# Hybrid encoder layer on one core: input projections in split halves, gate blocks between convolutions, a fixed order for the second sequence's queries, 80 up-blocks before the downs

## The chip, the cores and the metric

The kernel runs on one core of a Trainium2 chip. The metric is the device time of one execution in microseconds (us), lower is better, as the median of several executions. Engines: PE is TensorE (matmuls), DVE is VectorE, ACT is ScalarE, POOL is GpSimd, SP is SyncE, which here only issues DMAs.

## The reference

Two sequences of 256 tokens go through one encoder layer. Cut to what matters:

```python
h = layer_norm(concat([meta, x]))                 # 16 + 256 tokens, 1024 wide
proj = h @ w_in                                   # z | xBC | dt | c_q | c_kv | k_rope
y_ssm = rms_norm(ssd(silu(conv5(xBC)), dt) * silu(z))        # 16 heads, both directions
y_attn = rms_norm(attention(c_q @ w_uq, c_kv @ w_ukv, k_rope))  # 8 heads
h = layer_norm(alpha * h + concat([y_ssm, y_attn]) @ w_out)
# PEER: q = h @ w_q; 8 heads, product keys, top-16 twice, then
s1, s2 = q[..., 0] @ sub_keys[0].T, q[..., 1] @ sub_keys[1].T
experts, g = top16(top16(s1) + top16(s2))         # 16 of 16384 experts, softmax weights
act = gelu(u_tab[experts] . h);  out = sum(g * act * v_tab[experts])
y = layer_norm(alpha * h + out)[meta:]
```

All arrays are float32.

## The kernel before

**Two kinds of matmul.** `mm1` multiplies float32 tiles as they were loaded. `mm3` multiplies *halves*: a tile is split into a high half (an ACT cast to fp32r) and a low half (a DVE subtraction, raw minus high), and three fp32r matmuls, high by high, high by low, low by high, replace one float32 matmul. `stream` loads a 512 KB block of weights and splits it; its tiles are `wraw` (3 buffers), `whi` and `wlo` (2 each). `whole` loads a block for `mm1` into whichever of these seven buffers is next.

**First part.** Tokens are normalised and transposed into `hT` (channels on partitions, 272 columns). `win(s)` makes the input projections of sequence s: 18 blocks of w_in, eight accumulated matmuls each over 272 columns, and 8 half-blocks of w_z for the gates (4 chunks, 2 tiles of 256 columns each). Of the 18, 12 go through a five-tap convolution on DVE (four instructions at L415). `mla(s)` is the attention, `ssd(s)` the state-space part, `wout(s)` the output projection with the layer norm that follows, `queries(s)` the 16 query heads (projection, scores, `top16` on DVE). `mix` interleaves generators at fixed rates and the scheduler of the framework then orders each engine; the stages here are win(0) with mla(0), win(1) with ssd(0), wout(0) with mla(1) and ssd(1), queries(0) with the rest of these, and wout(1) with the routes of tiles 1 and 0 (`route`: a second top-16 and index arithmetic, nearly all DVE).

**Second part, in an order written by hand.** Of the four tiles of 128 tokens, tile 0 (`GT`) gathers its experts by indirect DMA (paced by `pace`, 257 gather steps in all, an accumulated rate per unit); tiles 1 to 3 (384 columns, `x1T_hi`, `x1T_lo`) instead go densely through all 16384 experts: an *up* (`umul`) multiplies 128 experts of u with the 384 tokens (24 fp32r matmuls and a gelu), a *down* (`outer`) multiplies their values with 128 experts of v. There are 128 of each. A `unit` is one step of the order: it may hold one up, and one hot step: a g step (`gunits`: 16 per tile, one-hot tables on DVE and 16 small f16 matmuls that build the dense gate matrix, written to DRAM as `gd`) or a route step (`rsteps`, 6 per tile). Up results of the first groups of 8 stay in SBUF (`RES` 2 groups) or are spilled to DRAM (`SPILL` groups, `hdr`). Before, the 16 g steps of tile 1 run with the 16 query heads of sequence 1 and an up in every second unit; then 6 route units, 16 g units, 6 and 16 again with an up each; then a flush, 12 more ups, and with 8 x (2 + 6) = 64 ups made, the loop of the downs starts with the other 64 ups inside.

Of the kernel before, what the change touches and what calls it, by code (L numbers as in the profile page):

```python
# [8 lines left out]
F32 = mybir.dt.float32  # L9
# [25 lines left out]
SPILL = 6  # L35
# [9 lines left out]
GDOWN, GUP = 0.8, 2.0  # L45
FIN = 116
EROWS, MRATE = 4, 0.8
HP = 400
RM, RS2, RM3, RS3 = 0.7, 0.6, 1.0, 0.6
# [3 lines left out]
DEL = (3, 0)  # L53
# [3 lines left out]
W0 = (12, 13, 14, 15, 16, 17, 8, 9, 10, 11, 0, 1, 2, 3, 4, 5, 6, 7)  # L57
W1 = (12, 8, 9, 13, 14, 15, 16, 17, 10, 11, 0, 1, 2, 3, 4, 5, 6, 7)
R0, RS = 1.05, 0.55
# [3 lines left out]
def build(ctx, tc, i, o):  # L63
# [176 lines left out]
    xbc, yn = [], []  # L240
    for _ in range(2):
        xbc.append(blk_tile([128, 12, L]))
        yn.append(blk_tile([128, 12, T]))
# [158 lines left out]

    def win(s):
        H = hT[s]
# [43 lines left out]
        for c in range(4):  # L448
            w = []
            for kh in range(2):  # L450
                w.append(whole(i["w_z"][2 * c + kh], 1024).rearrange("p (k m) -> p k m", k=4))
            for t in range(2):
                sl = slice(NM + t * 128, NM + (t + 1) * 128)
                pz = pm()[:, :256]
                mm1(pz, [(H[:, k, sl], w[k // 4][:, k % 4]) for k in range(8)])
                th = phw.tile([128, L], F32, name="th", bufs=2)[:, :256]
                nc.scalar.activation(th, pz, AF.Tanh, scale=0.5)
                zt = phw.tile([128, L], F32, name="cv")[:, :256]
                nc.vector.scalar_tensor_tensor(zt, th, 1.0, pz, op0=OP.add, op1=OP.mult)
                nc.sync.dma_start(zd[2 * s + t][:, c * 256:(c + 1) * 256], zt)  # L460
                yield 1

# [203 lines left out]

    def wout(s):
        kk = (8, 9, 10, 11, 0, 1, 2, 3, 4, 5, 6, 7)

        def prod(acc, t, n, w):  # L670
            k = kk[n]
            mm1(acc, [(yn[s][:, k, t * 128:(t + 1) * 128], w[:, (k % 2) * 512:(k % 2 + 1) * 512])], n_done=n, n_all=12)

        acc = [wa() for t in range(2)]
        for n in range(0, 12, 2):
            w = whole(i["w_out"][0, kk[n] // 2], 1024)
            for t in range(2):
                prod(acc[t], t, n, w)
                prod(acc[t], t, n + 1, w)
            yield 1  # L680
        h = blk_tile([128, 3, D])
        for t in range(2):
            nc.sync.dma_start(h[:, t], hd[2 * s + t])
        nc.scalar.dma_start(h[:, 2], bcast_row(i["ln1_g"], D))
        if s == 0:
            lq["b"] = gp.tile([128, D], F32, name="x1g")
            nc.scalar.dma_start(lq["b"], bcast_row(i["ln1_b"], D))
# [6 lines left out]
        for t in range(2):  # L694
            for n in range(12):
                prod(acc[t], t, n, ws[n // 2])
                if n % 4 == 3:
                    yield 1
# [581 lines left out]
```

## Time and profile before

| | |
|---|---|
| times | 1818.65, 1817.49, 1813.78 us; median 1817.49 |
| profiled execution | 1815.48 us, of which 1813.6 us is the span shown in the trace |
| PE busy | 1709.2 us (94%) |
| DVE busy | 1317.7 us (73%) |
| ACT busy, POOL busy | 639.0, 434.1 us |
| DMA | 433.83 MB, mean 239 GB/s |

The trace is one execution on one core. A busy PE is one that has matmuls in flight. The stages by their place in the span: 20.7 to 306 projections of both sequences, 306 to 357 wout(0), 357 to 511 the rest of attention and state space and the queries of sequence 0, 511 to 553 wout(1), 553 to 586 its norms and the routes of tiles 1 and 0, 586 to about 936 the 52 units with ups and the others, 936 to 1009 twelve ups and the passage to the downs, 1009 to 1750 the downs, then the finish.

### The profile page before, as it was taken

The page shows a single profiled execution, that of the slowest core. Times are in us where ns is not written, and L with a number is a line of the kernel's source. Part 1 is how long each engine was busy: PE and PEld are TensorE (multiplying, and loading weights), DVE is VectorE, ACT ScalarE, POOL GpSimd, SP SyncE. Part 2 cuts the span into 40 slices and gives each one's busy share as a digit, 9 for nine tenths or more (in the row PEclk, how much of TensorE's full clock was granted, in tenths as well). Part 3 has the DMA queues.
Part 4 walks back from the last instruction along what each step waited for, and adds up shares of the span by engine and source line. Part 5 has one row for each costly group of instructions (what it writes and reads, how often), then busy time and mean ns, then how long its engine had stood idle before and what let it go on. Part 6 is the DMA issues. An engine that isn't in the chain of part 4 may idle for free.

```text
span 1813.6 us, 24368 instructions
## 1 busy us (share of the span) xinstructions
PE 1709.2 (94%) x8860; PEld 1460.7 (81%) x8860; DVE 1317.7 (73%) x2821; ACT 639.0 (35%) x1153; POOL 434.1 (24%) x369
## 2 busy tenths in 40 slices
PE   7999999969995998998997999999999999999997
PEld 5788877548853997997996778899999999999885
DVE  5633484475579988989965577777787878787757
ACT  2313552064212334454543233333333333333332
POOL 0000133043000001110123112244454554545201
PEclk9999999989997999999998999999999999999999
DMA  8444245443332554585898899999999999998762
GB/s 302 151 152 128 95 161 157 155 121 107 116 131 86 180 209 163 204 319 176 322 345 310 310 326 307 343 354 339 335 310 330 339 310 335 340 315 319 254 220 93
DMA packets 178920, 433.83 MB, mean 239 GB/s; under 512 B 13505, under 2 KB 87681, under 8 KB 174193
## 3 DMA queue, kind: packets, MB, share of 16 engines
q1 hardware_dynamic: 135728, 259.14, 41.9%
q0 software_dynamic: 37024, 134.68, 21.0%
q10 hardware_dynamic: 6048, 38.47, 5.7%
q8 instruction: 69, 1.13, 0.3%
q14 instruction: 51, 0.41, 0.1%
HBM read 389.18 MB, written 43.06 MB: 238 GB/s over the span
## 4 chain that ended last, share of the span: by engine, by line
PE 77%; DVE 9%; DMA 7%; issue 3%; ACT 2%; SPq 1%; POOL 0%; ACTq 0%; POOLq 0%; DVEq 0%
PE bank L174 49%; PE bank L167 20%; DMA vraw<-in_v 3%; DMA R<-rd 2%; PE bank L861 1%; DVE wlo L1005 1%; PE bank L862 1%; PE bank L389 1%; PE bank L374 1%; DMA wraw<-in_uT 1%; DVE A L610 1%; SPq L1036 1%; DVE topp L781 1%; PE bank L383 0%; DVE topp L777 0%
## 5 line engine op out<-in xcount | busy, mean ns | idle before, releaser
L174 PE MATMUL bank<-x1T_hi,wlo 128*128 128x384 f32 x1024 | 345.2, 337 | 16.0 <-DVE wlo L1005 16.0
L174 PE MATMUL bank<-x1T_hi,whi 128*128 128x384 f32 x1024 | 348.0, 340 | 10.2 <-ACT whi L999 10.2
L174 PE MATMUL bank<-x1T_lo,whi 128*128 128x384 f32 x1024 | 343.4, 335 | 0.0
L174 PE MATMUL bank<-vhi,wh 128*128 128x512 f32 x756 | 296.0, 392 | 5.7 <-ACT wh L1053 5.7
L174 PE MATMUL bank<-vlo,wh 128*128 128x512 f32 x756 | 297.7, 394 | 1.4 <-DVE vlo L1054 1.4
L174 PE MATMUL bank<-vhi,wl 128*128 128x512 f32 x756 | 297.6, 394 | 0.0
L1054 DVE TENSOR_TENSOR vlo<-vraw,vhi 128x1024 fp32r<-128x1024 f32 x126 | 154.3, 1225 | 184.8 <-ACT vhi L1049 184.8
L950 POOL DMA_INDIRECT grow<-in_u,eidx x128 | 162.8, 1272 | 446.3 <-DVE grow L967 425.3
L1020 ACT ACTIVATE blk<-bank 128x384 f32<-128x384 f32 x128 | 62.8, 491 | 514.1 <-PE bank L174 514.0
L950 POOL DMA_INDIRECT grow<-in_v,eidx x128 | 186.1, 1454 | 193.1 <-DVE x1g L969 167.3
L174 PEld LDWEIGHTS bank<-x1T_hi,wlo 128*128 128x128 f32 x1024 | 192.5, 188 | 20.4 <-DVE wlo L1005 20.3
L174 PEld LDWEIGHTS bank<-x1T_hi,whi 128*128 128x128 f32 x1024 | 192.9, 188 | 13.2 <-ACT whi L999 10.5
L174 PEld LDWEIGHTS bank<-x1T_lo,whi 128*128 128x128 f32 x1024 | 192.8, 188 | 2.7
L1049 ACT CAST vhi<-vraw 128x1024 fp32r<-128x1024 f32 x126 | 131.8, 1046 | 158.3 <-issue 102.8
L1005 DVE TENSOR_TENSOR wlo<-wraw,whi 128x1024 fp32r<-128x1024 f32 x128 | 156.1, 1219 | 36.7 <-ACT whi L999 36.5
L174 PEld LDWEIGHTS bank<-vhi,wh 128*128 128x128 f32 x756 | 142.8, 189 | 35.5 <-ACT wh L1053 7.6
L174 PEld LDWEIGHTS bank<-vlo,wh 128*128 128x128 f32 x756 | 142.8, 189 | 31.5 <-DVE vlo L1054 3.0
L174 PEld LDWEIGHTS bank<-vhi,wl 128*128 128x128 f32 x756 | 142.9, 189 | 31.4 <-DVE wl L1055 1.5
L969 DVE SCALAR_TENSOR_TENSOR x1g<-grow,act,x1g 128x1024 f32<-128x1024 f32 x128 | 164.0, 1281 | 1.6
L967 DVE SCALAR_TENSOR_TENSOR grow<-grow,x1g 128x1024 f32<-128x1024 f32 x128 | 154.1, 1219 | 0.0
L999 ACT CAST whi<-wraw 128x1024 fp32r<-128x1024 f32 x128 | 134.6, 1052 | 21.4 <-DMA wraw<-in_uT 12.8
L1055 DVE TENSOR_TENSOR wl<-w,wh 128x384 fp32r<-128x384 f32 x128 | 70.8, 553 | 0.0
(344 smaller groups left out, 2492.2 us busy)
## 6 DMA issues: line engine op xcount, KB each, us to landing
wraw<-in_uT SPq DMA_DIRECT2D x128, 512.0 KB, 4.8
vraw<-in_v SPq DMA_DIRECT2D x128, 512.0 KB, 5.1
gd<-stg ACTq DMA_DIRECT2D x24, 1024.0 KB, 5.1
stg<-gd SPq DMA_DIRECT2D x16, 1536.0 KB, 12.5
hdr<-blk ACTq DMA_DIRECT2D x6, 1536.0 KB, 10.3
blk<-hdr SPq DMA_DIRECT2D x6, 1536.0 KB, 12.3
R<-rd SPq DMA_DIRECT2D x16, 512.0 KB, 3.8
qraw<-in_w_q SPq DMA_DIRECT2D x16, 512.0 KB, 3.9
```

Source lines behind the costliest of these rows:

```text
L167: nc.tensor.matmul(out, a, b, start=(n == 0), stop=(n == n_all - 1))
L174: nc.tensor.matmul(out, a, b, start=(n == 0), stop=(n == n_all - 1))
L374: nc.tensor.matmul(ps[:, :L], qT[:, t * 128:(t + 1) * 128], kT[:, h], start=True, stop=True)
L950: nc.gpsimd.indirect_dma_start(out=rows[n], out_offset=None, in_=i["uv"[n // 128]], in_offset=bass.IndirectOffsetOnAxis(ap=eidx[:, n % 128 ...
L967: nc.vector.scalar_tensor_tensor(r, r, 1.0, x1g, op0=OP.mult, op1=OP.mult, accum_out=act[:, k:k + 1])
L969: nc.vector.scalar_tensor_tensor(x1g, r, act[:, k:k + 1], x1g, op0=OP.mult, op1=OP.add)
L999: nc.scalar.copy(hi, ur[c])
L1005: nc.vector.tensor_tensor(lo, ur.pop(c), uw[c][0], op=OP.subtract)
L1020: nc.scalar.activation(hblk[c // 8][:, c % 8], pu, AF.Gelu)
L1049: nc.scalar.copy(hi, raw)
L1054: nc.vector.tensor_tensor(lo, raw, hi, op=OP.subtract)
L1055: nc.vector.tensor_tensor(wl, w, wh, op=OP.subtract)
```

## The change

1. In `win` and in the gates, `whole` and `mm1` become `stream(..., nc.vector)` and `mm3`; `hT` becomes a pair of halves, written by `transpose_split`, and the low half of each takes one of the four buffers named `blk`.
2. The gate chunks move into the order tables W0 and W1 as "z0" to "z3", between convolutions, in a generator `gate` of its own. mla(1) is mixed into win(1) already (`RM1`).
3. `queries(0)` handles only 13 heads in its stage. wout(1), its norms and transposes, heads 13 to 15 of sequence 0, the queries of sequence 1 and the routes of tiles 1 and 0 stand in one hand-written order.
4. The 16 units of the query heads hold 6 route steps of tile 1, 5 of tile 0 and five g steps, and each has an up. `merge` spreads the remaining 11 g steps of tile 1 among the route steps of tile 2, and the g steps of tile 2 among the route steps of tile 3.
5. `SPILL` is 8, so 80 ups come before the downs and 48 among them. The gather rates go from 0.8 to 1.0 per unit and from 0.8 to 0.9 per down.

```diff
-SPILL = 6
+SPILL = 8
-GDOWN, GUP = 0.8, 2.0
+GDOWN, GUP = 0.9, 2.0
-EROWS, MRATE = 4, 0.8
+EROWS, MRATE = 4, 1.0
-RM, RS2, RM3, RS3 = 0.7, 0.6, 1.0, 0.6
+RM, RS2, RM3, RS3, Q0 = 0.6, 0.6, 1.0, 0.7, 13
-W0 = (12, 13, 14, 15, 16, 17, 8, 9, 10, 11, 0, 1, 2, 3, 4, 5, 6, 7)
+W0 = (12, 13, 14, 15, 16, 17, 8, 9, "z0", 10, 11, "z1", 0, 1, "z2", 2, 3, "z3", 4, 5, 6, 7)
-    hT = [q.tile([128, 8, L], F32, name=f"hT{s}") for s, q in ((0, pha), (1, phb))]
+    hT = [(q.tile([128, 8, L], F32R, name=f"hT{s}"), blk.tile([128, 8, L], F32R, name="blk", bufs=4))
+          for s, q in ((0, pha), (1, phb))]
@@ def gate(s, c), def win(s)
+            w.append([x.rearrange("p (k m) -> p k m", k=4) for x in stream(i["w_z"][2 * c + kh], 1024, nc.vector)])
+            mm3(pz, [(H[:, k, sl], Lo[:, k, sl], w[k // 4][0][:, k % 4], w[k // 4][1][:, k % 4]) for k in range(8)])
-            w = whole(i["w_in"][u], 1024).rearrange("p (k m) -> p k m", k=8)
+            hi, lo = (x.rearrange("p (k m) -> p k m", k=8) for x in stream(i["w_in"][u], 1024, nc.vector))
-            mm1(pt, [(w[:, k], H[:, k]) for k in range(8)])
+            mm3(pt, [(hi[:, k], lo[:, k], H[:, k], Lo[:, k]) for k in range(8)])
@@
-    mix(w1, (sd0, RS))
+    mix(w1, (sd0, RS), (mla1, RM1))
-    mix(queries(0), (mla1, RM3), (sd1, RS3))
+    mix(queries(0, Q0), (mla1, RM3), (sd1, RS3))
-    r = chain((route, 1), (route, GT))
-    mix(wout(1), (r, 1.0))
@@ the hand-written order
+        for t in range(2):
+            wo.add(t, 1)
+            wo.norm(t)
+        uload(0)
+        uload(1)
+        wo.turn(0)
+        qproj(0, Q0)
+        qproj(0, Q0 + 1)
+        qtop(0, Q0)
+        wo.turn(1)
+        qtop(0, Q0 + 1)
+        qproj(0, Q0 + 2)
...
         qproj(1, 0)
         usplit(0)
-        for h, u in enumerate(gunits(1)):
+        g1 = gunits(1)
+        for h, u in enumerate(rsteps(1) + rsteps(GT, 5) + g1[:5]):
             qload(h + 2)
             qtop(1, h)
             qproj(1, h + 1)
-            unit(u, 0.0, h % 2)
+            unit(u, 0.0, first=u[1] is None)
-        for t in (2, 3):
-            for u in rsteps(t):
-                unit(u, 0.0, first=True)
-            for u in gunits(t):
-                unit(u, MRATE)
+        for u in merge(g1[5:], rsteps(2)) + merge(gunits(2), rsteps(3)) + gunits(3):
+            bank["f"] = wide
+            unit(u, 0.0 if u[1] is None else MRATE, first=u[1] is None)
@@
         gload(0)
+        for n in range(2):
+            unit(nop, 1.0)
         for c in range(RAWS - 1):
             vload(c)
```

On VectorE, in win(1), the changed program has a split of a weight block (`wlo`) beside each convolution. First the rows of the changed program: L436 is a tap of the convolution, L417 and L440 the gate and the convolution's last product.

```order
L417 SCALAR_TENSOR_TENSOR cv<-th,bank_1482 128x256
L152 TENSOR_TENSOR wlo<-wraw,whi 128x1024 x2
L436 SCALAR_TENSOR_TENSOR cv<-bank_1538,chans,cv 128x270
L436 SCALAR_TENSOR_TENSOR cv<-bank_1538,chans,cv 128x271 x2
L436 SCALAR_TENSOR_TENSOR cv<-bank_1538,chans,cv 128x270
L152 TENSOR_TENSOR wlo<-wraw,whi 128x1024
L436 SCALAR_TENSOR_TENSOR cv<-bank_1607,chans,cv 128x270
L440 SCALAR_TENSOR_TENSOR blk<-th,cv 128x272
```

Before, the convolutions there stand with pieces of the state-space part among them and nothing of a weight block (L415 is the tap, L419 the convolution's last product, L635 and L610 belong to ssd(0)):

```order
L415 SCALAR_TENSOR_TENSOR cv<-bank_1834,chans,cv 128x271 x2
L415 SCALAR_TENSOR_TENSOR cv<-bank_1834,chans,cv 128x270
L419 SCALAR_TENSOR_TENSOR blk<-th,cv 128x272
L415 SCALAR_TENSOR_TENSOR cv<-bank_1924,chans,cv 128x270
L415 SCALAR_TENSOR_TENSOR cv<-bank_1924,chans,cv 128x271 x2
L415 SCALAR_TENSOR_TENSOR cv<-bank_1924,chans,cv 128x270
L635 TENSOR_TENSOR y_1434<-bank_1478,y_1434 128x512
L419 SCALAR_TENSOR_TENSOR blk<-th,cv 128x272
```

What moved: 52 subtractions of 128x1024 elements (`wlo`) came into this engine's queue, each ahead of the matmuls that read it, and the gates (L417) stand among the convolutions.

The second place is VectorE at the end of wout(1). Before, the addition of the second product's tile (L700) and its layer norm (L205 to L188) stand between the steps of the routes of tiles 1 and 0 (L777 to L821):

```order
L187 TENSOR_SCALAR nr<-nr 128x1
L777 MAX_INDEX topp<-tops,cand 128x8 x7
L700 SCALAR_TENSOR_TENSOR blk<-blk,bank_4158 128x512
L821 TENSOR_TENSOR lq<-lq 128x8x128
L780 MAX tops<-c_4185 128x8
L188 TENSOR_TENSOR nr<-nr 128x1
L205 BN_STATS ln_st<-blk 128x6
L821 TENSOR_TENSOR lq<-lq 128x8x64
```

In the changed program nothing of a route stands there; the routes begin some fifty rows later, in the units. There, at the first unit, VectorE's queue reads (L751 to L756 are the top-16 of a query head, which stand there twice, for two tiles, L1043 splits a block of u, L805 begins a route step):

```order
L751 MAX tv_3541<-bank_5279 128x8
L752 MAX_INDEX ti_3545<-tv_3541,bank_5279 128x8
L754 MATCH_REPLACE S_5290<-tv_3541,bank_5279 128x128
L755 MAX tv_3541<-S_5290 128x8
L756 MAX_INDEX ti_3545<-tv_3541,S_5290 128x8
L1043 TENSOR_TENSOR wlo<-wraw,whi 128x1024
L805 TENSOR_TENSOR cand<-tv_3539 128x8x16 x5
```

What moved: of the 16 units of the query heads, 11 now hold a top-16 of two tiles, one split and one route step in this engine's queue, and 5 hold a g step in the route step's place.

## Rows read from the trace of the kernel before

**Rows 1.** Page: the chain that ended last, its shares of the span by engine.

```profile
PE 77%; DVE 9%; DMA 7%; issue 3%; ACT 2%; SPq 1%; POOL 0%; ACTq 0%; POOLq 0%; DVEq 0%
```

**Rows 2.** Windows: length, busy PE PEld DVE ACT POOL, PE's clock, DMA share, GB/s.

```profile
20.67:165.00 144.33, 143.25 (x672) 118.42 (x673) 68.15 (x204) 37.35 (x88) 1.49 (x3) 1.00 0.53 176
165.00:306.00 141.00, 135.57 (x683) 108.41 (x682) 80.62 (x236) 67.17 (x188) 36.65 (x44) 0.96 0.41 131
...
357.00:410.00 53.00, 38.02 (x176) 26.63 (x176) 41.26 (x106) 32.91 (x99) 23.04 (x24) 0.87 0.40 122
...
511.00:553.00 42.00, 42.00 (x110) 19.47 (x109) 31.76 (x177) 2.58 (x3) 0.20 (x1) 1.00 0.34 111
553.00:586.00 33.00, 13.22 (x41) 9.31 (x40) 32.35 (x130) 11.24 (x14) 0.20 (x1) 0.64 0.14 55
...
854.00:930.00 76.00, 76.00 (x601) 73.64 (x600) 70.85 (x102) 36.71 (x59) 15.31 (x12) 1.00 0.90 326
930.00:1009.00 79.00, 63.69 (x339) 59.66 (x336) 38.82 (x53) 23.81 (x34) 24.02 (x18) 0.91 0.92 329
...
1200.00:1690.00 490.00, 490.00 (x2479) 446.15 (x2479) 394.09 (x452) 165.14 (x237) 238.67 (x166) 1.00 0.93 325
```

**Rows 3.** Line L167, projection matmuls: count, minimum/median/maximum ns, first and last start.

```profile
L167 PE MATMUL bank<-hT,wraw x240: 392/392/742, 20.7 to 258.3; 128*128 128x272 f32 x120
...
L167 PE MATMUL bank<-wraw,hT x128: 379/379/483, 104.6 to 302.5; 128*128 128x256 f32 x128
```

**Rows 4.** Chain of waits, three stretches: start us, us, what (xcount instructions).

```profile
166.41 1.29 PE bank L389 x12
...
192.68 3.67 PE bank L167 x16
...
590.91 3.46 PE bank L167 x16
594.37 4.18 PE bank L174 x24
...
599.46 0.50 PE bank L757 x4
```

**Rows 5.** Chain of waits, a stretch of downs alone (512 columns).

```profile
1694.80 45.25 PE bank L174 x205
```

**Rows 6.** Page, groups: busy us, mean ns, idle before and what ended it.

```profile
L174 PE MATMUL bank<-x1T_hi,wlo 128*128 128x384 f32 x1024 | 345.2, 337 | 16.0 <-DVE wlo L1005 16.0
...
L1005 DVE TENSOR_TENSOR wlo<-wraw,whi 128x1024 fp32r<-128x1024 f32 x128 | 156.1, 1219 | 36.7 <-ACT whi L999 36.5
...
L967 DVE SCALAR_TENSOR_TENSOR grow<-grow,x1g 128x1024 f32<-128x1024 f32 x128 | 154.1, 1219 | 0.0
...
L999 ACT CAST whi<-wraw 128x1024 fp32r<-128x1024 f32 x128 | 134.6, 1052 | 21.4 <-DMA wraw<-in_uT 12.8
```

**Rows 7.** Chain of waits by line, 355 to 420 us.

```profile
by line: DMA R<-rd 38.5%; PE bank L167 10.2%; ACT A L609 8.3%; DVE A L610 7.0%; PE bank L580 5.5%; DMA rd<-A 5.1%; DVE Dm L612 4.2%; issue 2.4%; PE bank L389 1.9%; PE bank L623 1.6%; PE bank L383 1.5%; PE bank L619 1.4%; DVE qT L371 1.3%; P
```

**Rows 8.** DVE groups, 20 to 511 us: a quarter of a layer norm's scaling.

```profile
L217 DVE SCALAR_TENSOR_TENSOR blk<-blk,ln_mv 128x512 f32<-128x512 f32 x4 | 2.8, 744 | 0.0
```

**Rows 9.** DVE timeline, 595 to 603 us: start of a top-16 pair, g step, next top-16.

```profile
595.34 0.29 DVE L715 MAX8 tv<-bank 128x8 f32<-128x128 f32 x1
...
598.51 0.67 DVE L848 TENSOR_TENSOR ohb<-iotaR,ijT 128x1024 f16<-128x1024 f16 x1
...
602.29 0.29 DVE L715 MAX8 tv<-bank 128x8 f32<-128x128 f32 x1
```

**Rows 10.** DVE timeline, one route, its first and last instruction.

```profile
699.46 1.10 DVE L769 TENSOR_TENSOR cand<-tv 128x128 f32<-128x128 f32 x5
...
732.09 0.42 DVE L832 TENSOR_TENSOR ijT<-bank,ijT 128x256 f16<-128x256 f32 x1
```

**Rows 11.** Chain of waits, passage to the downs.

```profile
984.34 21.95 DMA vraw<-in_v
...
1008.75 19.81 PE bank L174 x78
```

More of the change, by code (lines that the diff above doesn't have):

```diff
@@ L238, in blk_tile @@
         return blk.tile(shape, F32, name="blk", bufs=4)
[L240 to L243, printed above, removed]
+    xbc = [blk_tile([128, 12, L])]
+    yn = [blk_tile([128, 12, T])]
     misc = [ph.tile([128, L], F32, name="misc0")]
@@ L447, in win @@
             yield 1
[L448 to L461, printed above, removed]
     def step(gen, n=1):
@@ L665, in build @@
     lq = {}
-    def wout(s):
[L668 to L687, printed above, removed]
+    KK = (8, 9, 10, 11, 0, 1, 2, 3, 4, 5, 6, 7)
@@ L688, in wout @@
+    def wout(s):
+        o = Wout(s, wa, at)
+        yield from o.first()
+        o.rows()
         with tc.high_priority(offset=HP):
             for t in range(2):
-                nc.vector.scalar_tensor_tensor(h[:, t, :512], h[:, t, :512], ALPHA, acc[t], op0=OP.mult, op1=OP.add)
-        acc = [wa() for t in range(2)]
-        ws = [whole(i["w_out"][1, kk[n] // 2], 1024) for n in range(0, 12, 2)]
-        xf = None
+                o.add(t, 0)
+        o.load2()
         for t in range(2):
[L695 to L698, printed above, removed]
+            yield from o.second(t)
@@ L711, in wout @@
+                o.norm(t)
+                o.turn(t)
             yield 1
@@ L720, in top16, with queries @@
         nc.vector.max_index(ix[:, 8:16], v[:, 8:16], S2)
-    def queries(s):
-        for hh in range(16):
+    def queries(s, n):
+        for hh in range(n):
             key = rt2.tile([128, 128], F32, name="key")
@@ L1098, in build @@
     pace.acc = 0.0
-    r = chain((route, 1), (route, GT))
-    mix(wout(1), (r, 1.0))
-    step(r, 100)
     sst.close()
-    x1g = gp.tile([128, D], F32, name="x1g")
-    nc.sync.dma_start(x1g, x1d[GT])
     phase(5)
@@ L1137, in unit, with rsteps, merge @@
         pace(rate)
-    def rsteps(t):
+    def rsteps(t, n=6):
         g = route(t)
-        return [(lambda: step(g), None) for _ in range(6)]
-    with tc.manual_schedule():
+        return [(lambda: step(g, 7 if t == GT and k == n - 1 else 1), None) for k in range(n)]
+    wide = banks(2, 3, 4, 5, 6, 7)
+    def merge(a, b):
+        out, k = [], 0
+        for n, u in enumerate(a):
+            while k < len(b) and k * len(a) <= n * len(b):
+                out.append(b[k])
+                k += 1
+            out.append(u)
+        return out + b[k:]
+    with tc.manual_schedule():
+        wo = Wout(1, banks(0, 1, 2, 3), banks(4, 5, 6, 7))
+        wo.rows()
+        for _ in wo.first():
+            pass
+        wo.load2()
+        for h in range(Q0, 16):
+            qload(h)
+        for t in range(2):
+            wo.add(t, 0)
+        for t in range(2):
+            for _ in wo.second(t):
+                pass
+        qbank, pbank = banks(0, 1), banks(2, 3)
+        for t in range(2):
+            wo.add(t, 1)
[9 more added lines that the diff above has]
+        qproj(0, Q0 + 2)
         qload(0)
         qload(1)
+        qtop(0, Q0 + 2)
+        x1g = gp.tile([128, D], F32, name="x1g")
+        nc.sync.dma_start(x1g, x1d[GT])
+        qbank, pbank = banks(2, 3), banks(4, 5)
         qproj(1, 0)
-        uload(0)
-        uload(1)
         usplit(0)
-        for h, u in enumerate(gunits(1)):
+        g1 = gunits(1)
+        for h, u in enumerate(rsteps(1) + rsteps(GT, 5) + g1[:5]):
             qload(h + 2)
```

99 lines of the change are left out of this document (77 added, 22 removed).

## Prediction, made before the changed kernel ran

> **What bounds the kernel now.** I read the page first: PE holds 77% of the chain that ended last, DVE 9%, DMA 7% [rows 1]. So time is won by taking work from PE or by filling its gaps, and DVE is the engine that could object. The windows then say where each holds. The reader is to see three kinds of stage in them [rows 2]. In the projections (20.7 to 306 us) PE is busy for 278.8 of 285.3 us with DVE at 148.8. From 357 to 410 and from 553 to 586 PE starves and its granted clock falls (0.87 and 0.64), with DVE busy for 32.35 of 33 us in the second. From 854 to 930 and in the downs PE is full, DVE at 80 to 93% (394.09/490 and 70.85/76) and the DMA share at 0.90 to 0.93.
>
> The sum is made against the profiled execution, 1815.5 us, of which the trace's span is 1813.6; the median of the runs is 2.0 us above it, and I add that at the end. Differences under 0.3% (5.5 us) a measurement here can't tell from none.
>
> **A. Projections on PE.** Removed: 576 instructions of 272 columns (240 with `wraw`, 176 and 160 with the two other tiles) and 256 of 256 columns (128 and twice 64) [rows 3], which is 36 units and 16 half-chunks of 16 instructions. In the chain 16 of them take 3.67 and 3.46 us [rows 4]. Added: 24 fp32r matmuls each. No row has fp32r at these widths. 384 columns take 4.18/24 = 174 ns, 512 columns 45.25/205 = 221 ns [rows 4, 5]; at 2.4 GHz, the upper clock level, the columns alone are 160 and 213 ns, so 8 to 14 ns are overhead. The nearest floor is a run of small matmuls bound by their weight loads, 1.29/12 = 107 ns [rows 4], below 272 columns (113 ns) and level with 256. I take columns plus 13.5 ns: 127 and 120 ns, 3.04 and 2.88 us per 24. PE is spared 36 x 0.63 + 16 x 0.58 = 32 us. Bounds: at columns alone 36 x 0.95 + 16 x 0.90 = 49 us spared; at the price of 384 columns (4.18) 36 x 0.51 + 16 x 0.72 = 30 us more.
>
> The row says that a float32 matmul of 272 columns takes 3.67/8 = 459 ns, four times 115 ns [rows 4]. The Trainium skill, "FP8 and Floating Point Precision", section "TensorE Precision Notes", counts true FP32 as four passes through the array; by that, three passes would cost three quarters, 2.75 and 2.60 us, and 47 us would be spared; after the halving of B that is 8 us off the forecast, inside its band. The rows of fp32r make me keep 32, because each of the 24 instructions pays its own overhead.
>
> **B. What the halves cost on DVE, ACT and in the order.** 52 blocks (36 and 16) get an ACT cast and a DVE subtraction at 1.05 and 1.22 us [rows 6]: 63 us of DVE. Before, DVE had 148.8 busy of 285.3 us [rows 2]; after, 212 of about 253, 84%. The average hides the uneven part: convolutions come in runs, four taps and two products near 0.5 us each beside a split, so in these runs DVE needs about as long as the PE does. mla(1), moved into win(1), brings more DVE work there. PE's cover is thus thin and I let half of the 32 us go: 16 us are left. Behind a `wlo` that waits for its cast stand taps, whose products ACT, the transposes and ssd wait for: that is the way in which a late split would spread. The loads can run only three raw blocks ahead instead of seven, which the DMA share of 0.41 to 0.53 in these stages allows [rows 2]. Four small items: the first projection waits for the subtraction of hT and may wait for the split of its first weight block (1 us and 1.05 + 1.22, +3); the gates stand where DVE has little else, nothing; the pairs of buffers held longer, nothing, for the ups already live with two `whi` and two `wlo` and waited only 16.0 us for `wlo` over 128 ups [rows 6]. The fourth is the hole at 357 to 410: 15 us of idle and a low clock, and 38.5% of the chain there is the round trip of ssd(1)'s decay rows through DRAM [rows 2, 7]. mla(1) used to fill it and is now partly gone, but the queries start earlier; I take -9 for a shorter chain with less competition for DVE. Bounds -20 (hole gone) and +10 (less filler, same chain). Section: -16 + 3 - 9 = -22.
>
> **C. From wout(1) to the first down.** Before: 511 to 1008.75 us [rows 11], 498 us with 64 ups and 48 g steps. The changed stretch holds 16 more ups (16 x 4.18 = 67 us that leave the downs) and three more query heads (3 x (3.46 + 0.5) = 12 us that leave queries(0)), so it breaks even at 577. Step by step:
> - wout(1): 41 us of PE (96 instructions of 512 columns; the window of 42 us holds a few of other lines) [rows 2].
> - Then nothing of a route stands in DVE's way, but an addition and a norm (four passes over half a tile at 0.744 [rows 8], two of statistics about as long, the addition, and a dozen one-column steps at an estimated 0.15: 7 us), splits of the transposes (estimated at 4 x 0.65), top-16s of three heads (3.2 each: 595.34 to 598.51 is two tiles [rows 9]) and the first split stand in a row before the first up: about 20 us, with three projections of PE (10 us) under them. Before, 33 us went by there.
> - 16 units: PE needs 3.46 + 0.5 + 4.18 = 8.1 (a head with its scores, then an up [rows 4]). DVE needs top-16 3.2, a split of 1.2 [rows 6] and a route step. A route took 33 us from 699.46 to its last end at 732.5, with five splits inside: 27 in six steps [rows 10]; I take 27 for tile 1 and 25 for tile 0, whose last pieces are left to a later step, 4.75 each. DVE: 9.15 for 11 units; 5 more with a g step in the route step's place, at PE's 8.1 + 0.9 of f16 matmuls: 146 us.
> - A unit of a g step and an up has 40 matmuls, 24 and 16; 601 in 76 us [rows 2] make 15 units at 5.1. On DVE it is four tables and a split (598.51 to 602.29, 3.8 [rows 9]) and up to a gather of 1.2 with its read of the sum, 5.1 as well. A route unit is 4.5 + 1.2 on DVE, 4.18 on PE. 17 units (11 and 6): 11 x 5.1 + 6 x 5.7 = 90. 22 units (16 and 6): 116. The last 16 g units: 82.
> - 9 ups and the passage: 38 us, and 15 for what stood open before, where the last wait was for a v block (21.95 [rows 11]) and PE was busy for 63.7 of 79 us at clock 0.91 [rows 2]. Two ups now stand between the gate block's load and the v loads on SP's queue, and their uT blocks no longer wait behind these.
> Sum 41 + 20 + 146 + 90 + 116 + 82 + 53 = 548, 29 below 577. Bounds: -45 (passage closed, units on PE alone) and 0 (a DVE unit 1 us longer over the 39 and no gain at the norms).
>
> **D. Downs.** 16 fewer ups there (counted in C). 56 downs instead of 40 now run without an up; the 40 already kept PE full at a DMA share of 0.93 [rows 2]. Two more groups of 1.5 MB are written and read back: 6.3 MB at 325 GB/s are 19 us of transfers, behind PE as long as the share stays under 1. Gathers at 1.0 instead of 0.8 per g unit: 326 GB/s x 76 us over 15 units is 1.65 MB per unit, plus 0.2 of 512 KB is 1.76 MB in 5.1 us, 345 GB/s, share 0.95 [rows 2]. I charge +3 for bursts. Bounds 0 and +20.
>
> Sum: -22 - 29 + 3 = -48; 1815.5 - 48 + 2 = 1769.5, and I give **1769 us**.
>
> **The rivals.** R1, DVE eats the whole saving of A (0 instead of 16, and nothing from the hole): for it, two thirds of the blocks sit beside convolutions; against, DVE's mean of 84%. 1815.5 + 3 - 29 + 3 + 2 = 1794 us. Chance 0.2.
>
> R2, the scheduled g units and the downs become bound by DMA. If 326 GB/s [rows 2] is a ceiling, 1.76 MB take 5.4 us instead of 5.1: 43 gather units x 0.3 = 13, and up to 10 more in the downs; 1792. Against: 0.90 is not 1, and before, PE never waited in that window. Chance 0.15.
>
> R3, the other side: each split stands open before its matmuls. A cast and a subtraction are 1.05 + 1.22 us [rows 6]; if DVE's queue is so full that no block is ready when PE comes to it, 52 x 2.27 = 118 us are added: 1815.5 - 32 + 118 + 3 - 29 + 3 + 2 = 1881. It ends slower once an exposed block costs over (32 + 29 - 3 - 3 + 5.5)/52 = 1.2 us on average. Against: 16 us over 128 ups [rows 6], 0.13 each. Chance 0.05.
>
> R4, fp32r at short widths is bound by something that makes it as dear as 384 columns: PE gets 30 us more in place of 32 less; 1769 + 16 + 30 = 1815, no change. Against: the 107 ns row [rows 4]. Chance 0.05.
>
> R5, more than I take: no DVE limit in the projections, all of the 32 us and the hole: 1815.5 - 32 + 3 - 15 - 36 (C with 7 less) + 2 = 1738. Chance 0.15. The rest, 0.4, is my forecast, within 12 us of 1769.
>
> **How the numbers follow.** 1769 is the likeliest case. R1 and R2 reach to 1794, R5 to 1738; R3 and R4 and their like are left out at the top with 0.1, and what goes beyond R5 at the bottom with about as much: 1738 to 1798. Faster by over 5.5 us: the forecast, R1, R2, R5, together 0.9; R4 falls on both sides of 1812: same 0.04, slower 0.06.
>
> **What would show it.** Right: the 24 matmuls of a projection take near 3.0 us in the chain where nothing interrupts them; PE's busy time falls by about 30 us in total; the span from the first projection to the start of wout(1) shrinks by 25 to 40 us, with DVE above 80% and some idle of PE put down to `wlo` or to a convolution; from the end of wout(1) to the first up some 20 us; the 16 units at about 9.1 us with DVE full; the first down some 30 us earlier than 1008.75 + 67 less what the first part gave. Wrong: projections near 4 us; PE idle on `wlo` for more than 60 us; a DMA share at 1.0 in the units with idle put down to uT or v blocks.

## The result, and the profile after

The changed kernel takes 1844.44 us (median of 1837.54 to 1848.41) against 1817.95 for the kernel before in the same runs: ratio 1.0147, 95% interval 1.0111 to 1.0182. It is slower by 1.5%, where I forecast 2.7% faster. Its profiled execution took 1848.4 us, the span is 1846.3.

The page of the changed kernel, the engines' busy time and the last chain's shares by engine (the second row answers to [rows 1]), then two groups of matmuls (the first of them answers to the first of [rows 6]):

```profile
PE 1711.9 (93%) x9276; PEld 1495.7 (81%) x9276; DVE 1391.0 (75%) x2883; ACT 694.6 (38%) x1209; POOL 419.1 (23%) x371
...
PE 72%; DVE 15%; DMA 6%; ACT 4%; issue 2%; ACTq 0%; POOL 0%; SPq 0%; DVEq 0%; POOLq 0%
...
L174 PE MATMUL bank<-x1T_hi,wlo 128*128 128x384 f32 x1024 | 354.4, 346 | 47.6 <-DVE wlo L1043 47.6
L174 PE MATMUL bank<-x1T_hi,whi 128*128 128x384 f32 x1024 | 358.7, 350 | 4.7 <-ACT whi L1037 4.7
```

PE's share of the chain fell from 77 to 72%, DVE's rose from 9 to 15. The wait of the ups for `wlo`, 16.0 us before, is 47.6. Windows of the changed kernel, in the columns of [rows 2]:

```profile
20.67:165.00 144.33, 135.09 (x949) 127.69 (x950) 108.77 (x252) 69.48 (x129) 1.74 (x5) 0.94 0.50 167
165.00:306.00 141.00, 128.98 (x813) 112.00 (x813) 98.26 (x247) 83.30 (x205) 40.97 (x44) 0.90 0.40 123
...
357.00:410.00 53.00, 49.85 (x217) 32.51 (x216) 44.38 (x125) 31.16 (x95) 21.34 (x22) 0.94 0.45 149
...
741.00:803.00 62.00, 48.72 (x312) 46.81 (x312) 42.84 (x71) 26.12 (x35) 6.47 (x7) 0.89 0.59 204
803.00:854.00 51.00, 45.24 (x304) 43.67 (x305) 42.26 (x107) 18.12 (x28) 6.78 (x6) 0.93 0.71 244
854.00:930.00 76.00, 62.06 (x402) 59.76 (x401) 53.98 (x91) 31.02 (x43) 8.34 (x9) 0.89 0.63 221
```

The hole at 357 is nearly closed (49.85 of 53 us busy, 38.02 before). From 741 to 930 it is the reverse of what I expected: PE is busy for about 82%, its granted clock is near 0.9, and no other engine is full, neither DVE (about 74%) nor the DMA queues (0.59 to 0.71, where I feared 0.95). When nothing is full and everything waits, a chain runs back and forth between engines.

Where it lies is seen from the ups, each of which ends in a gelu on ScalarE. The times between successive gelus, read off ScalarE's timeline (start of the first in us, then differences):

```
before   ups 16 to 32, g steps:                5.1 each
         ups 9 to 14, one route:               8.0 4.2 6.7 6.4 6.8 5.5
changed  ups 2 to 17 (first at 566.6):         8.1 8.1 8.1 8.1 8.1 8.5 25.6 10.6 8.1 8.1 8.1 8.1 9.0 9.0 5.6 7.1
         ups 18 to 31 (g and route steps):     5.1 8.1 5.1 5.1 7.3 5.1 5.4 12.2 5.1 5.1 11.2 5.1 5.1 10.7
         ups 44 to 51:                         11.3 5.1 5.1 12.5 5.2 5.1 5.1 12.0
```

Two things stand out, one up that came 25.6 us after the one before, and a late up at the route steps of the merged list. Against the steps of the prediction:

```
                                     predicted    profile
end of wout(1), to an equal work     -22          -13   (528.8 - 554.0 + 12 for the three heads)
end of wout(1) to the first up        20           33   (528.8 to 562.0)
16 units of the query heads          146          148   (gelu 1 to gelu 17)
39 merged units                      206          254   (gelu 17 to gelu 56)
the last 16 g units                   82           83   (gelu 56 to gelu 72)
9 ups and the passage                 53           50   (start of up 72, 4.6 us before its gelu, to the first down, 1097.0)
the first two downs                    0           11   (1097.0 to the third down, 1108.0; in no step of the sum)
downs from there, to an equal work    +3           +1   (738.3 against 804.9 - 67.5)
```

The differences, 9 + 13 + 2 + 48 + 1 - 3 + 11 - 2, add up to 79 of the 81 us between the forecast -48 and the +33 of the spans. The first is the least sure: wout(1) ended at 521.5 to 528.8 us in kernels that are alike up to there.

The two downs have a row because the 1008.75 of [rows 11], which I took for the first down, is the second matmul of the third. TensorE's timeline in the kernel before has the first matmul of the first down, and the first two of the third:

```profile
995.65 0.50 PE L174 MATMUL bank<-vhi,wh 128*128 128x512 f32 x1 [2.44 <-ACT wh L1053]
...
1007.90 0.50 PE L174 MATMUL bank<-vhi,wh 128*128 128x512 f32 x1 [1.71 <-ACT wh L1053]
1008.75 0.49 PE L174 MATMUL bank<-vlo,wh 128*128 128x512 f32 x1 [0.34 <-DVE vlo L1054]
```

and in the changed kernel the first down's first matmul and the same place of the third down:

```profile
1097.01 0.49 PE L174 MATMUL bank<-vhi,wh 128*128 128x512 f32 x1 [2.44 <-ACT wh L1091]
...
1108.02 0.39 PE L174 MATMUL bank<-vlo,wh 128*128 128x512 f32 x1
```

**The up that came 25.6 us late.** VectorE's timeline in the changed kernel, around up 8 (L805 begins a route, L861 ends the route of tile 0, L1043 is the split of an up's block):

```profile
615.76 1.22 DVE L1043 TENSOR_TENSOR wlo<-wraw,whi 128x1024 fp32r<-128x1024 f32 x1
616.90 1.09 DVE L805 TENSOR_TENSOR cand<-tv 128x128 f32<-128x128 f32 x5
...
642.95 0.29 DVE L861 SCALAR_TENSOR_TENSOR eidx<-ij 128x128 int32<-128x128 f32 x1
...
646.33 1.21 DVE L1043 TENSOR_TENSOR wlo<-wraw,whi 128x1024 fp32r<-128x1024 f32 x1
```

and TensorE's at the same place, with the idle time ahead of an instruction and what ended it:

```profile
638.91 1.22 PE L793 MATMUL bank<-qkey,qs 128*128 128x128 f32 x4 [15.39 <-ACT qs L788]
```

The whole route of tile 0 runs in one unit, 26 us, and 29 us pass between two splits. The code says why: `rsteps(GT, 5)` makes five functions in a loop, meant to run one step each and the rest in the last (`7 if t == GT and k == n - 1 else 1`), but each reads `k` when it is called, and then `k` is 4 in all of them. The first unit runs everything and four run nothing. I had read that line as it was meant.

**The late ups of the merged list.** Three timelines of the changed kernel at one of them, ScalarE, VectorE, TensorE:

```profile
750.63 0.49 ACT L1058 ACTIVATE blk<-bank 128x384 f32<-128x384 f32 x1 [2.08 <-PE bank L174]
751.09 1.08 ACT L900 ACTIVATE stg<-bank 128x512 f32<-128x512 f32 x2
752.20 1.28 ACT L822 ACT_TABLE_LOAD   x1
753.49 0.31 ACT L822 ACTIVATE cand<-cand 128x128 f32<-128x128 f32 x1
```

```profile
749.73 0.29 DVE L821 TENSOR_TENSOR cand<-tops 128x128 f32<-128x128 f32 x1
753.83 0.29 DVE L824 TENSOR_REDUCE sm<-cand 128x8 f32<-128x128 f32 x1 [3.82 <-ACT cand L822]
...
757.50 0.68 DVE L884 TENSOR_TENSOR ohb<-iotaR,ijT 128x1024 f16<-128x1024 f16 x1
...
760.16 1.22 DVE L1043 TENSOR_TENSOR wlo<-wraw,whi 128x1024 fp32r<-128x1024 f32 x1
```

```profile
755.74 0.34 PE L174 MATMUL bank<-x1T_lo,whi 128*128 128x384 f32 x1
761.43 0.69 PE L174 MATMUL bank<-x1T_hi,wlo 128*128 128x384 f32 x1 [5.36 <-DVE wlo L1043]
```

The route step on VectorE (L821) needs an exponential from ScalarE, whose queue first holds the gelu of the running up (L1058) and the evictions of its f16 matmuls (L900): the answer comes at 753.8, 3.82 us of waiting. Then the step goes on for 3.7 us, the four tables of the next g step follow (L884 and three more, 2.7), and only then the split that TensorE's next up but one needs. From 751.3, when its f16 matmuls ended, to 761.4 TensorE had one up to cover 10.1 us: it idled for 5.36. Thirteen waits of this kind are 44.8 us from 710 to 968.

### The profile page after: what moved, and what is told of

The parts are those of the page before. It is cut to its first block, busy times and chain, and to the rows that moved or that the text cites. A ratio compares the mean times of both kernels' runs of the same rounds, so it can differ in the third digit from the quotient of the medians.

```text
span 1846.3 us, 25386 instructions
## 1 busy us (share of the span) xinstructions
PE 1711.9 (93%) x9276; PEld 1495.7 (81%) x9276; DVE 1391.0 (75%) x2883; ACT 694.6 (38%) x1209; POOL 419.1 (23%) x371
## 4 chain that ended last, share of the span: by engine, by line
PE 72%; DVE 15%; DMA 6%; ACT 4%; issue 2%; ACTq 0%; POOL 0%; SPq 0%; DVEq 0%; POOLq 0%
PE bank L174 56%; PE bank L167 9%; DMA vraw<-in_v 2%; DMA R<-rd 2%; DVE wlo L1043 2%; DMA wraw<-in_uT 1%; PE bank L897 1%; PE bank L898 1%; PE bank L391 1%; PE bank L376 1%; DVE lq L857 1%; DVE topp L817 1%; DVE wlo L152 1%; DVE lq L855 1%; DVE topp L813 1%
## 5 line engine op out<-in xcount | busy, mean ns | idle before, releaser
L174 PE MATMUL bank<-x1T_hi,wlo 128*128 128x384 f32 x1024 | 354.4, 346 | 47.6 <-DVE wlo L1043 47.6
L174 PE MATMUL bank<-x1T_hi,whi 128*128 128x384 f32 x1024 | 358.7, 350 | 4.7 <-ACT whi L1037 4.7
L174 PE MATMUL bank<-x1T_lo,whi 128*128 128x384 f32 x1024 | 351.7, 343 | 0.0
L988 POOL DMA_INDIRECT grow<-in_u,eidx x128 | 143.9, 1124 | 633.2 <-DVE grow L1005 596.6
L1058 ACT ACTIVATE blk<-bank 128x384 f32<-128x384 f32 x128 | 62.8, 491 | 513.5 <-PE bank L174 513.5
L174 PEld LDWEIGHTS bank<-x1T_hi,wlo 128*128 128x128 f32 x1024 | 199.6, 195 | 52.7 <-DVE wlo L1043 52.7
L174 PEld LDWEIGHTS bank<-x1T_hi,whi 128*128 128x128 f32 x1024 | 199.3, 195 | 7.6 <-ACT whi L1037 5.3
L1043 DVE TENSOR_TENSOR wlo<-wraw,whi 128x1024 fp32r<-128x1024 f32 x128 | 156.1, 1219 | 62.0 <-ACT whi L1037 61.9
L174 PEld LDWEIGHTS bank<-x1T_lo,whi 128*128 128x128 f32 x1024 | 199.1, 194 | 2.2
L174 PEld LDWEIGHTS bank<-vhi,wl 128*128 128x128 f32 x756 | 142.5, 189 | 31.2 <-DVE wl L1093 1.6
L174 PE MATMUL bank<-hT,whi 128*128 128x272 f32 x288 | 89.0, 310 | 5.0 <-DVE cv L520 3.4
## 6 DMA issues: line engine op xcount, KB each, us to landing
stg<-gd SPq DMA_DIRECT2D x16, 1536.0 KB, 11.7
```

Source lines behind the costliest of these rows:

```text
L174: nc.tensor.matmul(out, a, b, start=(n == 0), stop=(n == n_all - 1))
L988: nc.gpsimd.indirect_dma_start(out=rows[n], out_offset=None, in_=i["uv"[n // 128]], in_offset=bass.IndirectOffsetOnAxis(ap=eidx[:, n % 128 ...
L1043: nc.vector.tensor_tensor(lo, ur.pop(c), uw[c][0], op=OP.subtract)
L1058: nc.scalar.activation(hblk[c // 8][:, c % 8], pu, AF.Gelu)
```

## The experiments

Every kernel was timed beside the kernel before on the same chip; ratios are against that. "Gain" is against the changed kernel's 1844.4 or the kernel named. The kernel before took 1813.9 to 1818.0 us in the five groups of runs, so a gain between kernels of different groups is uncertain by some 4 us.

**e1_spread.** The step number is bound when the list is made.

```diff
-return [(lambda: step(g, 7 if t == GT and k == n - 1 else 1), None) for k in range(n)]
+return [(lambda k=k: step(g, 7 if t == GT and k == n - 1 else 1), None) for k in range(n)]
```

> One edit: in rsteps the step number is bound when the list is made, so that the route of tile 0 runs one step per unit over five units; in the changed kernel the function reads the number after the loop, which is 4 in every unit, so the first of the five does all steps. Theory (the route stands whole in one unit, 26 us of VectorE between two top-16s, up 8 comes 25.6 us and up 9 10.6 us after the one before instead of 8.1): all ups of the first 16 units come 8 to 9.2 us apart, and about 18 us are saved, 1844 to 1826 (1820 to 1832). Rival (VectorE bounds these 16 units whichever way its work is spread): the ups after it come at over 9.2 us each and less than 6 us are saved.

1831.7 us, ratio 1.0087 (1.0062 to 1.0111), a gain of 12.7. The 25.6 and 10.6 us are gone, but ups 9 to 13 now come 8.3, 9.8, 9.5, 8.6 and 13.1 us apart: VectorE has 135.9 busy of 150 us from 562 to 712. So the cause is right, at two thirds of the size. That VectorE is the bound of these units, as the rival has it, explains only a part of the missing third: the 13.1 stand where the first g step's tables (2.7 us) come ahead of the split. With the split first (c2_all_split_first below) that up comes 8.9 us after the one before, and the 16 units take 130.8 us, against 137.0 here and 148.1 in the changed kernel.

**e2_nomerge.** The list without the merge.

```diff
-for u in merge(g1[5:], rsteps(2)) + merge(gunits(2), rsteps(3)) + gunits(3):
+for u in g1[5:] + rsteps(2) + gunits(2) + rsteps(3) + gunits(3):
```

> One edit: merge is left out, so that 11 g units, 6 route units, 16 g units, 6 route units and 16 g units follow each other. Theory (a route step asks ScalarE for an exponential or a copy that stands behind the gelu and the evictions of the up before it, VectorE waits for the answer, and in the merged list the tables of the next g step stand ahead of the next block's split, 10.3 us against 4.2 us of TensorE work): the ups of the g units come 5.1 us apart and those of the route units 6.2 on average as in the kernel before, so the 39 units take 213 us instead of 254 and the time falls by about 40 to 1804 (1797 to 1815). Rival (the merged stretch is slow because of gathers at 1.0 or the memory): no change within 8 us, since work and transfers stay.

1798.3 us, ratio 0.9904 (0.9877 to 0.9931), a gain of 46.1: this edit alone makes the changed kernel faster than the one before. The 39 units take 209.0 us instead of 253.7, with the same instructions and transfers. The windows of this kernel and, below, of the changed one:

```profile
712.00:950.00 238.00, 224.73 (x1600) 215.41 (x1599) 221.95 (x437) 112.48 (x164) 40.07 (x34) 0.99 0.77 272
```

```profile
712.00:968.00 256.00, 212.85 (x1389) 204.68 (x1388) 194.52 (x399) 98.70 (x142) 27.84 (x28) 0.91 0.62 213
```

Clock and DMA share rise with the pace: the low DMA share was an effect of the waits.

**e3_split_first.** The merged list, with the hot step behind the next block's split in every unit from there on.

```diff
-unit(u, 0.0 if u[1] is None else MRATE, first=u[1] is None)
+unit(u, 0.0 if u[1] is None else MRATE, first=True)
```

> One edit: from the merged list on, every unit has its hot step behind the split of the next block (first is True for g units too). The round trip through ScalarE stays, but the tables, 2.7 us, no longer stand ahead of the split. Theory of the round trip with the tables behind it: each of the ten late ups comes about 2.7 us and some clock earlier, 25 to 35 us are saved, 1844 to 1814 (1805 to 1824). Rival (the wait for ScalarE alone is the loss, or the tables are needed as early as the split): less than 10 us, or slower, since the f16 matmuls then wait for the tables.

1809.1 us, ratio 0.9968 (0.9952 to 0.9984), a gain of 35.3. The ten late ups come 4.2 to 8.4 us after the one before instead of 7.3 to 12.5, and the waits for `wlo` in that stretch fall from 44.8 to 20.0 us. The tables ahead of the split were most of the loss; the 2.7 us that they take count for more, since TensorE's mean clock is higher as well (0.97 from 712 to 950, against 0.91).

**c3_ahead_of_gelu.** On top of e3_split_first, in units of a route step the split and the step stand ahead of the up and its gelu.

```diff
-if not first:
+route = fill is None and cu < 72
+if c is not None and route:
+    ulow(c + 1)
+if not first or route:
     hot()
 if c is not None:
     umul(c)()
 while late:
     late.pop()()
-if c is not None:
+if c is not None and not route:
     ulow(c + 1)
-if first:
+if first and not route:
     hot()
```

> The changed kernel with its merged list and its unbound step number, with the edit of e3_split_first, and in units of a route step the split and the route step issued ahead of the up and its gelu. It asks whether ScalarE's answer, which stood behind the gelu of the up, is the rest of the loss that e3_split_first left (35 of the 46 us of e2_nomerge were won there). Theory: the late ups, 6.2 to 8.4 us after the one before in e3_split_first, come 1 to 3 us earlier each, 8 to 20 us in all, 1795 (1789 to 1802). Rival (the sum of VectorE's work behind one up is what is late, wherever the answer stands): within 5 us of 1809.

1798.1 us, ratio 0.9887 (0.9861 to 0.9913), 11.0 less than e3_split_first. VectorE's waits for the exponential and the copies, 5.5 + 11.7 us there, are 3.4 + 0.5, the waits of the ups for `wlo` 6.6 us, and the 39 units take 202.6 us (216.3 in e3_split_first), below my 206. So the answer behind the gelu was the rest. The rival falls: the sum of the work on VectorE was not the bound. In the units of the query heads, which the edit also touches, it loses 2.6 us (150.7 against 148.1).

**e4_gather08.** The gathers of the g units back at 0.8.

```diff
-EROWS, MRATE = 4, 1.0
+EROWS, MRATE = 4, 0.8
```

> One edit: the gather rate of the g units back from 1.0 to 0.8. Rival theory (the DMA share or the gathers' VectorE time slow the merged units): the merged 39 units lose 10 to 25 us, time 1820 to 1834. Theory of the round trip: within 6 us of 1844, since a gather less on VectorE every fifth unit takes 1.3 us from a chain of which it is no part in most units.

1845.7 us, ratio 1.0162 (1.0129 to 1.0194): no change. The gathers were not what slowed the merged units.

**b1_both.** The edits of e1_spread and e2_nomerge together.

> The two edits of e1_spread and e2_nomerge together. If the whole route in one unit and the merged list are two causes in two places, their gains add: 1844.4 - 12.7 - 46.1 = 1786 (1780 to 1792), faster than the kernel before by 1.3 to 1.8%. If the one hid the other: 1794 or more.

1787.6 us, ratio 0.9822 (0.9784 to 0.986). The two gains, 12.7 and 46.1, add up to 58.8; measured 56.8, the same within the 4 us. They are two causes in two places.

**b2_float32.** b1_both with the projections back in float32 (leaving the order tables and the mixing as changed).

```diff
-hi, lo = (x.rearrange("p (k m) -> p k m", k=8) for x in stream(i["w_in"][u], 1024, nc.vector))
+w = whole(i["w_in"][u], 1024).rearrange("p (k m) -> p k m", k=8)
... (likewise for the gates; hT is one float32 tile)
-mm3(pt, [(hi[:, k], lo[:, k], H[:, k], Lo[:, k]) for k in range(8)])
+mm1(pt, [(w[:, k], H[:, k]) for k in range(8)])
```

> On top of b1_both, the projections and gates back in float32: hT one tile, weights loaded whole, mm1 in place of mm3; order tables, mixing and everything behind them stay. It asks what the halves are worth here. The prediction's sections A and B (24 fp32r matmuls at 3.01 us against 3.67, half of the 32 us kept): about 16 slower than b1_both, 1802 (1794 to 1812). Rival 1 (VectorE eats it all): the same as b1_both within 5 us. Rival 2 (PE bounds everything there): 30 slower, 1816.

1800.6 us, ratio 0.9908 (0.9873 to 0.9943), 13.0 slower than b1_both. The halves are worth 13 us here where I gave 16 less 3 for the start; both rivals fall. In the two traces wout(1) ends 9.4 us earlier with halves (526.4 against 535.8); the other few us are within the scatter of the runs. The windows of b1_both, then of b2_float32, show where the other part of the 32 us may have gone:

```profile
20.67:165.00 144.33, 135.22 (x952) 127.80 (x953) 108.73 (x251) 69.79 (x129) 1.73 (x5) 0.94 0.50 167
165.00:306.00 141.00, 129.21 (x814) 112.05 (x813) 98.40 (x247) 83.37 (x204) 41.19 (x44) 0.90 0.40 124
```

```profile
20.67:165.00 144.33, 142.90 (x669) 117.83 (x670) 68.41 (x198) 35.16 (x81) 1.27 (x1) 1.00 0.53 177
165.00:306.00 141.00, 136.12 (x705) 110.43 (x704) 79.22 (x228) 72.41 (x201) 36.60 (x47) 0.98 0.39 123
```

With halves PE idles for 20.9 us in these 285 (6.3 without), and its clock is 0.94 and 0.90 (1.00 and 0.98 without): some 15 us go to idle. That the rest goes to the lower clock fits, but no run separates the two, and the windows do not hold quite the same work.

**b3_gathers_later.** b1_both with fewer gathers per down and more per up behind.

```diff
-GDOWN, GUP = 0.9, 2.0
+GDOWN, GUP = 0.6, 2.7
```

> On top of b1_both, fewer gathers in downs (0.6 instead of 0.9 per down) and more with the ups (2.7 instead of 2.0). Question: why 56 downs alone take 4.36 us each, where 40 took 4.22 before and 18 matmuls at 0.221 are 3.99. Theory (the memory is the bound there): the 56 downs take 4.1 to 4.25 us each, 6 to 14 us are won there, of which the downs with ups, which then carry more gathers, give back up to half. Rival (they wait for something else, a v block's split or the spill's reload): 4.36 stays, no change within 4 us.

1780.7 us, ratio 0.9789 (0.9749 to 0.9829), 6.9 less. From the first down to the start of up 81, 57 downs, it takes 234.8 us against 245.0: 4.12 us a down instead of 4.30 (4.22 in the changed kernel). The profiled execution of b1_both is a long one there: in the eight kernels with 1.0 in the units and 0.9 in the downs the stretch takes 240.4 to 246.1 us, in the five with 0.6 it takes 234.6 to 236.0. The windows, up to the gelu of up 81, b1_both first:

```profile
1040.00:1289.00 249.00, 243.34 (x1050) 198.30 (x1051) 186.07 (x281) 84.96 (x115) 52.62 (x52) 0.99 0.93 327
```

```profile
1038.00:1277.00 239.00, 238.66 (x1051) 197.88 (x1052) 167.47 (x247) 84.28 (x115) 37.11 (x36) 0.99 0.89 307
```

The DMA share falls to 0.89 and PE's idle from 5.7 us to nearly none. That fewer gathers make the downs alone shorter is shown; whether as transfers or as 34 fewer instructions on VectorE, this run doesn't tell apart. The question had a false start: 4.36 and 4.22 don't count the same downs. Counted alike, without the waits at the start, the changed kernel takes 4.18 us a down (56 downs behind the first) and the kernel before 4.17 (38 behind the third).

**b4_banks.** b1_both with the queries of sequence 1 in banks 4 and 5 and their scores in 2 and 3.

```diff
-qbank, pbank = banks(2, 3), banks(4, 5)
+qbank, pbank = banks(4, 5), banks(2, 3)
 qproj(1, 0)
```

> On top of b1_both, the queries of sequence 1 are projected into PSUM banks 4 and 5 and scored in 2 and 3, instead of the other way. Theory (between the end of wout(1) and the first up, 33 us where I gave 20, the first query of sequence 1 waits for a bank in which the top-16 of the last head of sequence 0 still reads): the projection starts some 6 us earlier, the first up 4 to 6 us earlier, 1781 if b1_both is 1786. Rival (VectorE's row of norms and top-16s sets the first up): under 2 us.

1779.0 us, ratio 0.9783 (0.9748 to 0.9817), 8.6 less. TensorE's timeline in b1_both at that projection:

```profile
549.39 6.66 PE L167 MATMUL bank<-blk,qraw 128*128 128x256 f32 x16 [3.73 <-DVE S L754]
```

It waits for a top-16 that still reads the bank (L754), and then 16 matmuls take 6.66 us where the next sixteen take 3.62: the granted clock from 549.39 to 556.05 is 0.55, behind 3.73 us of idle. In b4_banks the wait is not there, and from the end of wout(1) to the first up it takes 27.1 us instead of 34.0. That is 6.9 where I expected 4 to 6, since the clock came on top; the rest of the 8.6 stands ahead of it or is scatter.

**c1_all, c2_all_split_first, f1_merged_ahead.** c1_all joins b1_both, b3_gathers_later and b4_banks; c2_all_split_first adds to it `first=True` for all units; f1_merged_ahead brings back the merge with the order of c3_ahead_of_gelu in the merged part alone.

In c2_all_split_first (the units of the query heads; the list behind them likewise):

```diff
-unit(u, 0.0, first=u[1] is None)
+unit(u, 0.0, first=True)
```

In f1_merged_ahead, with the other lines of c3_ahead_of_gelu and the merged list:

```diff
+route = fill is None and cu < 72 and bank["f"] is wide
```

> The edits of b1_both, b3_gathers_later and b4_banks together. They sit in four places of the span, so I expect the sum: 1787.6 - 6.9 - 8.7 = 1772 (1766 to 1779), 2.4% faster than the kernel before. If the earlier first up only moves a wait: 1778 or more.

> c1_all with the split of the next block ahead of the hot step in every unit, g units and units of the query heads too. Theory (a split that stands behind other work is late): the ups that are late in b1_both, the thirteenth (14.3 us after the one before) and those behind the first route step, come 3 to 6 us earlier, 5 to 12 us in all, 1764. Rival (the g units need their tables as early): the g units go from 5.1 to over 5.3 us each and the gain is gone, 1772 or more.

> c2_all_split_first with the merged list back and, in its units of a route step, the split and the route step issued ahead of the up and its gelu, as in c3_ahead_of_gelu. There the 39 units from up 17 to up 56 took 202.6 us, in b1_both and its like 207 to 209. If the merge loses only by the order inside a unit, it now wins: 4 to 7 us faster, 1760. Rival (the DMA share, 0.95 in these units once nothing else is late): 1766 or more.

1773.6 (0.9755, 0.9729 to 0.9781), 1766.3 (0.9728, 0.9703 to 0.9753) and 1761.5 us (0.9688, 0.9665 to 0.971), all three in their ranges. c2's thirteenth up comes 8.9 us after the one before (14.3 in b1_both). It wins 7.3 us in the 16 units of the query heads (130.8 against 138.1 in c1_all) and loses 4.5 in the 39 units (212.3 against 207.8): the g units stay at 5.1, against its rival, but some units about the route steps take over 8. In f1_merged_ahead the 39 units take 204.0 us, less than the unmerged list in either order. Of the last steps each is about as large as the intervals; c1 to f1 is not. f1_merged_ahead beats both kernels: 3.1% below the one before.

**d1_mla_later.** c2_all_split_first with mla(1) out of win(1).

```diff
-mix(w1, (sd0, RS), (mla1, RM1))
+mix(w1, (sd0, RS))
```

> c2_all_split_first without mla(1) in win(1): the second sequence's attention starts beside wout(0) as in the kernel before; halves, gates and all the rest stay. It asks why the part up to wout(1) gave 12 us where I forecast 22. If the attention's steps in win(1) take VectorE and the weight queue from the projections (one load waits 28.3 us there): 4 to 10 us faster, 1759, wout(1) ends earlier. Rival (they fill PE where ssd waits for DRAM, and without them the hole behind wout(0) opens again): 4 to 12 us slower, 1774.

1797.5 us, ratio 0.9896 (0.9879 to 0.9912), 31.2 slower: my theory for this one falls, and the rival is right at three times its size. wout(1) ends at 554.9 instead of 521.5, and from 357 to 410 PE is busy for 39.2 us (48.9 in c2) at a clock of 0.84 (0.97 in c2).

## Why the prediction was wrong

**Section C failed, at its fourth bullet.** I costed a merged unit as the larger of PE's and DVE's sums, 5.1 for a g step and 5.7 for a route step. The sum of the 39 units, 206, was right: c3_ahead_of_gelu runs the same list in 202.6 us. What I left out, and so put at nothing, is the order inside the unit: VectorE runs at most one block ahead (two `whi`, two `wlo`), so what stands between two splits must fit under one up. Before, a route unit was followed by another, whose split came first; the merge set a g unit there, whose tables stand first, behind a route step that waits for ScalarE. The runs show the price: 254 us instead of 206, of which 37 go with the tables behind the split (e3_split_first, 216.3) and 14 more with the step ahead of the gelu (c3_ahead_of_gelu). The kernel before showed a trace of it that I averaged away, route units at 6.4 to 6.8 beside 4.2.

**Its third bullet was right by luck.** 146 forecast, 148 measured, but 26 us of route stood in one unit. Without that, the first 16 units are shorter than I said, 137.0 in e1_spread: ups 2 to 7 came at 8.1, TensorE's time, with a route step each, and not at my 9.15.

**The second bullet, 20 us, was 33.** VectorE's row took 24 us (528.8 to 553.0). But TensorE's three projections did not fit under it: it idled for 3.10 us until VectorE had read a bank, and from 552.3 to 562.0 it projected two heads before the first up, the first in 5.39 us at a granted clock of 0.68, the second in 3.62. b4_banks took 7 us of such a stretch back.

**Section A held, and section B as far as the runs tell.** 24 matmuls of 272 columns take 3.01 us (forecast 3.04), in the changed kernel's chain:

```profile
108.41 3.01 PE bank L174 x24
```

The row's price stands, then. The Trainium skill, "FP8 and Floating Point Precision", section "TensorE Precision Notes", counts true FP32 as four passes; the estimate worked out from that, 2.75 us for three passes, is not what this trace has.

Of the 32 us 13 were kept (b2_float32), with a start later by the 3 us forecast (first projection at 23.67): the 16 less 3 of the sum. The hole was given at -9; up to the end of wout(1) the whole came to -13 and not -22 here, and to -15 to -21 in the other kernels that are alike up to there. The section's sum is thus off by 1 to 9 us, and its small size hides large terms: mixing mla(1) into win(1) alone wins 31 us (d1_mla_later), and without it wout(1) ends at 554.9, 13 us later than in the kernel before at equal work. So other parts of the change cost more than the halves win. Whether these are the order tables, the late buffers, the two steps by which mla(1) now starts later (`DEL`) or the mixing rates is open.

**The fifth bullet and section D held; two downs stood in neither.** The passage ended at the first down, 50 us where I gave 53, and the downs from the third on cost +1 where I forecast +3. Between the two the changed kernel spends 11 us, which no step of the sum had, since I read the third down of the kernel before as its first. Its nine ups and passage took 52.8 us (942.8 to 995.65), and not 65.9: of the 13 us that I saw to win there, 8 were the work of two downs. The gathers take some 6 us of the downs alone (b3_gathers_later), but as a gain that was left, and no loss against the kernel before. For the g units they were no bound (e4_gather08).

PE's busy time, one of my signs, was to fall by about 30 us. It rose from 1709.2 to 1711.9, with ups at the lower clock in it; in f1_merged_ahead, where these are gone, it is 1676.3.

None of the rivals was what happened. R3 came nearest, splits that stand open before their matmuls, but I looked for it among the 52 blocks of the projections; it happened to the blocks of the ups, at ten places, because of what was put into VectorE's queue ahead of them.

## What to carry to other kernels

When units of several engines are merged, don't add up the engines' times alone: write down the queue of each engine between two hand-overs, and ask what stands ahead of the instruction for which the busiest engine waits, and where a round trip to another engine and back fits. With buffers two deep, the longest unit decides and not the mean. And read a list of functions made in a loop as it runs when called, not as it is written.

## What the runs showed of the hardware

A short wait cost more than itself. After TensorE had idled for 5.36 us in the changed kernel, the next up was slow; the chain shows it against an undisturbed up shortly before:

```profile
746.37 4.22 PE bank L174 x24
...
761.43 6.79 PE bank L174 x22
```

The window of that up has a granted clock of 0.50 (the last three numbers of a row are the clock, the DMA share and GB/s), that is the lower of the two levels, 1.2 GHz:

```profile
761.00:766.00 5.00, 4.57 (x14) 4.57 (x15) 4.93 (x8) 0.00 (x0) 1.15 (x1) 0.50 0.57 165
```

At 4.22 us for 24, 22 matmuls take 3.9 us, so 2.9 are lost on top of the 5.4. This is one reason why the merged stretch lost 54 us over 5.1 per unit, with 44.8 us of waits, and why small edits (e3_split_first, b4_banks) gave more than the instructions that they moved.

ScalarE's change from gelu to exponential put a table load of 1.28 us into the round trip (752.20): it began 0.03 us after the copy ahead of it, and the exponential 0.01 us after it. The Trainium skill, "ScalarE: Activation LUTs", section "What ACT_TABLE_LOAD costs", has the same 1283 ns and adds a drain of about 1380 ns to each switch; no such gap stands in these rows.
